# First block: GLU and k projections 512 features wide, chunks loaded in two pieces, parameters on ScalarE's queue, sinks behind the first convolution input

## The chip, the cores and the metric

The kernel runs on one core of a Trainium2 chip. Its engines are TensorE (PE, matrix products), VectorE (DVE) and ScalarE (ACT) for elementwise work, GpSimd (POOL) and SyncE (SP); SP, ACT and POOL can issue DMAs. The metric is the device time in microseconds (us), median of three runs.

## What is computed

Two transformer blocks on x of 512 tokens by 1024 features, in float32. Only the first block's mixer is touched by the change:

```python
h = rms_norm(x, norm1_g)
proj = h @ w_in                      # 1024 x 2560
q, k, v, glu_a, glu_b = split(proj)  # 512 features each
q = rms_norm(q by head, q_norm_g); k = rms_norm(k by head, k_norm_g)
attn = stick_breaking_attention(q, k, v)        # 8 heads of 64
c = glu_a * sigmoid(glu_b)
c = causal_depthwise_conv(c, conv_dw_w, conv_dw_b)   # 31 taps
c = silu(layer_norm(c, conv_ln_g, conv_ln_b))
x = x + concat([attn, c]) @ w_out
```

After it come a gated feed-forward with a 3-tap convolution, then a second block with its own mixer (gated recurrence and sliding-window attention with sinks), a second gated feed-forward and a last norm. The sinks are read by the second block alone.

## The kernel before

Every product is made of float32r parts: a weight chunk arrives as `raw`, ScalarE casts it to `whi`, VectorE takes the rest as `wlo`; the normed input has parts `n_hi` and `n_lo`; `mm3` issues three matmuls for each pair (hi*hi, hi*lo, lo*hi). `WeightStream.load` issues the DMA on SP and records the two splits; there are 3 buffers for `raw` and 4 each for `whi` and `wlo`, and `get` loads up to three chunks ahead. Weights lie in memory in the order of use, which `weight_plan` makes.

A class `Recorder` records all instructions in program order and then orders them by list scheduling on estimated costs: each engine takes the first instruction in program order whose operands and buffers are there. The result is a fixed order for every engine's queue; on the chip each engine runs its queue in that order, so an instruction that waits holds all behind it. Tiles of one tag ("lane") share `BUFS` buffers: lane `x` has 8, lane `z` has 4 PSUM banks, `mm` 2, `o` 1.

The first block's steps stand in `ORDER1`: `glu0 glu1 k1 taps2 taps0 k0 q0 v conv0 stick0 q1 conv2 ...`. At the start SP loads x in eight tiles of 128 features (256 KB each), and `AFTER_X` says after which of them a weight chunk is recorded. `Norm.add` makes `n_hi` on ScalarE and `n_lo` on VectorE for each tile, scaled by `gain1`, a tile of 8 columns that ScalarE's own queue loads; the other parameters (`prm`, 361 columns, 180.5 KB) come later, on SP. `square` sums the squares for the norm.

`glu(c)` makes 256 of the 512 channels: `project_quarter` gives token-major halves, [128 tokens, 256 features] in half a PSUM bank, first for the gate (`glub`), then for the value (`glua`); sigmoid on ScalarE and a product on VectorE follow, four transposes (`gluT`) by channel tile, and a copy into `cpad` (ScalarE). `qk_quarter` does four heads of q or k in the same half-bank form: copies `tn`, squares, sums by head (`ms`), a reciprocal square root by logarithm and one Newton step (`u`, `r`), a product with `tn`, transposes, `qn`/`kn`.

The convolution has two helpers. `conv_taps` makes the first taps by ScalarE products `tap` that GpSimd adds by accumulating DMAs onto one tile per channel tile, 13 in a row for tiles 0 and 1 and 2 for tiles 2 and 3; each product lies in a buffer of lane `x` until its DMA has landed. `conv_pair` does the other taps on VectorE (`conv`), then adds the sums of the first. `stick_pair` (steps stick0 to stick3) needs `e` tiles, also of lane `x`: scores on PE (`z`), three activations, a maximum and split on VectorE (`sph`, `spl`), sums on PE, weighted values (`av`). `conv_norm` (`cmu`, `cvar`) ends the convolution path; then the output product `wo` starts with that part.

The sinks, 4 KB, are loaded by GpSimd:

```python
sink = cp.tile([P, 8], F32, name="sink")
G.dma_start(sink, sinks_2.partition_broadcast(P).rearrange("p o h -> p (o h)"))
```

It needs nothing, so its place is the start of GpSimd's queue.

## Time and profile before

| | |
|---|---|
| runs | 1208.17, 1208.4, 1210.71 us; median 1208.4 |
| span of the profiled execution, first to last instruction | 1205.9 us |
| TensorE busy | 1191.8 us, 6144 matmuls |
| VectorE busy | 761.3 us, 1288 instructions |
| ScalarE busy | 504.1 us, 795 instructions |
| GpSimd busy | 32.4 us, 85 instructions |
| weights and x on SP's queue | 105.65 MB |

The profile gives the span as the execution's only time; the median of the runs lies 2.5 us above it. All times below are us from the span's start unless they are durations. A matmul's busy time includes its flow through the array, so consecutive ones overlap; the distance of starts tells what one costs.

### The profile page before, as it was taken

What the parts mean: (1) busy time and instruction counts of PE and PEld (TensorE: products, weight loads), DVE (VectorE), ACT (ScalarE), POOL (GpSimd) and SP (SyncE); (2) the same over time, 40 slices, a digit from 0 to 9 for tenths busy, and PEclk for the clock granted to TensorE, in tenths of its full rate; (3) what the DMA queues carried; (4) which work ended last, traced back from release to release, by engine and by line L of the source; (5) the groups of instructions that cost most, each with busy time, mean ns of one, the idle gap of its engine ahead of it and who ended that gap; (6) DMA issues with size and microseconds to landing.
All of it is one profiled execution on the core that took longest, in us unless ns stands there. A gap on an engine that the chain in (4) does not pass through costs nothing.

```text
span 1205.9 us, 15657 instructions
## 1 busy us (share of the span) xinstructions
PE 1191.8 (99%) x6144; PEld 988.7 (82%) x6144; DVE 761.3 (63%) x1288; ACT 504.1 (42%) x795; POOL 32.4 (3%) x85
## 2 busy tenths in 40 slices
PE   9999999999999999999999999999999999999997
PEld 8998766888888888888889877778888888888886
DVE  6889885676653566355775667877666445653554
ACT  7286796453321233133544245655523223321324
POOL 0033100000000000000000000000000000000000
PEclk9999999999999999999999999999999999999999
DMA  7389421233232323322322222112332323232321
GB/s 235 106 181 200 92 88 35 77 99 105 88 105 88 105 90 103 92 96 79 118 70 72 70 78 68 49 61 79 105 100 92 104 89 105 88 105 89 103 71 70
DMA packets 36553, 116.09 MB, mean 96 GB/s; under 512 B 4224, under 2 KB 4352, under 8 KB 36480
## 3 DMA queue, kind: packets, MB, share of 16 engines
q1 hardware_dynamic: 31248, 105.65, 28.1%
q0 software_dynamic: 4512, 8.39, 4.0%
q8 instruction: 48, 0.79, 0.3%
q10 hardware_dynamic: 720, 1.05, 0.2%
q14 instruction: 25, 0.20, 0.1%
HBM read 105.12 MB, written 2.10 MB: 89 GB/s over the span
## 4 chain that ended last, share of the span: by engine, by line
PE 94%; DMA 3%; DVE 1%; ACT 1%; issue 0%; SPq 0%; ACTq 0%; POOLq 0%
PE d L266 20%; PE g L266 20%; PE u L266 20%; PE wo L266 7%; PE z L266 4%; DMA tap<-tap 2%; PE hi L266 2%; PE glub L266 2%; PE hg L266 2%; PE glua L266 2%; PE hq L266 2%; PE hf L266 2%; PE aq L266 2%; PE hl L266 2%; PE av L266 1%; PE k0ps L266 1%
## 5 line engine op out<-in xcount | busy, mean ns | idle before, releaser
L266 ACT CAST whi<-raw 128x1024 fp32r<-128x1024 f32 (+2 forms) x194 | 200.8, 1035 | 475.2 <-PE d L266 152.1
L266 DVE TENSOR_TENSOR wlo<-raw,whi 128x1024 fp32r<-128x1024 f32 (+2 forms) x194 | 233.0, 1201 | 93.7 <-ACT whi L266 93.4
L266 PE MATMUL g<-n_hi,whi 128*128 128x512 f32 x352 | 137.2, 390 | 0.0
L266 PE MATMUL g<-n_hi,wlo 128*128 128x512 f32 x352 | 137.1, 390 | 0.0
L266 PE MATMUL g<-n_lo,whi 128*128 128x512 f32 x352 | 137.1, 389 | 0.0
L266 PE MATMUL u<-n_lo,whi 128*128 128x512 f32 x352 | 137.0, 389 | 0.0
L266 PE MATMUL u<-n_hi,whi 128*128 128x512 f32 x352 | 137.0, 389 | 0.0
L266 PE MATMUL u<-n_hi,wlo 128*128 128x512 f32 x352 | 137.0, 389 | 0.0
L266 PEld LDWEIGHTS u<-n_hi,whi 128*128 128x128 f32 x352 | 66.1, 188 | 13.8
L266 PEld LDWEIGHTS u<-n_hi,wlo 128*128 128x128 f32 x352 | 66.1, 188 | 13.7
L266 PEld LDWEIGHTS g<-n_hi,wlo 128*128 128x128 f32 x352 | 66.1, 188 | 13.7
L266 PEld LDWEIGHTS g<-n_hi,whi 128*128 128x128 f32 x352 | 66.1, 188 | 13.7
L266 PEld LDWEIGHTS u<-n_lo,whi 128*128 128x128 f32 x352 | 66.1, 188 | 13.6
L266 PEld LDWEIGHTS g<-n_lo,whi 128*128 128x128 f32 x352 | 66.1, 188 | 13.5
L266 DVE TENSOR_TENSOR s<-s,u 128x512 f32<-128x512 f32 x44 | 30.3, 688 | 67.1 <-PE u L266 67.1
L266 DVE TENSOR_TENSOR gp<-g,n__rstd 128x512 f32<-128x512 f32 x44 | 30.4, 692 | 63.9 <-PE g L266 63.8
L266 PE MATMUL d<-wlo,f_hi 128*128 128x512 f32 (+1 forms) x182 | 69.5, 382 | 0.0
L266 PE MATMUL d<-whi,f_lo 128*128 128x512 f32 (+1 forms) x182 | 69.5, 382 | 0.0
L266 PE MATMUL d<-whi,f_hi 128*128 128x512 f32 (+1 forms) x182 | 69.5, 382 | 0.0
L266 PE MATMUL d<-f_hi,whi 128*128 128x512 f32 x176 | 68.5, 389 | 0.0
L266 PE MATMUL d<-f_lo,whi 128*128 128x512 f32 x176 | 68.5, 389 | 0.0
L266 PE MATMUL d<-f_hi,wlo 128*128 128x512 f32 x176 | 68.5, 389 | 0.0
(389 smaller groups left out, 2388.6 us busy)
## 6 DMA issues: line engine op xcount, KB each, us to landing
raw<-in_weights_dram SPq DMA_DIRECT2D x182, 512.0 KB, 3.6
tap<-tap POOLq DMA_DIRECT2D x30, 256.0 KB, 4.7
raw<-in_weights_dram SPq DMA_DIRECT2D x8, 384.0 KB, 3.1
xin<-in_x_dram SPq DMA_DIRECT2D x8, 256.0 KB, 6.2
xres<-in_x_dram SPq DMA_DIRECT2D x8, 256.0 KB, 3.4
raw<-in_weights_dram SPq DMA_DIRECT2D x4, 256.0 KB, 5.7
out_dram<-hts ACTq DMA_DIRECT2D x4, 256.0 KB, 2.8
out_dram<-hts SPq DMA_DIRECT2D x4, 256.0 KB, 2.6
```

Of the source, the lines that this page charges most:

```text
L266: getattr(self.engines[op.queue], method)(*op.args, **op.kw)
```

## The change

The GLU becomes one product 512 features wide for each `c`: 256 columns of the gate and 256 of the value side by side, in four full PSUM banks of lane `z`, for both `c`. A chunk then consists of two pieces that lie apart in the weights, each with a DMA, a cast and a subtraction of its own into halves of one `whi` and one `wlo` tile. `GLU` sets the chunks: for `glu0` one 128-row block each for the first two, then two each; for `glu1` two each. `raw` still has 3 buffers, now counted in pieces. k becomes one product of 512 features (chunks of two blocks, as v has), with one norm over 32 columns where there were two over 16; q stays in quarters. `ORDER1` has `k` in place of `k1`, and no `k0`. The whole of `prm` is loaded first, on ScalarE's queue, in place of `gain1`, and SP's later load of it is gone. `AFTER_X` goes from (0, 2, 4, 6) to (0, 1, 3, 5). The sinks' DMA waits for the first `cpad` tile. The tiles `sq` go from lane `t` to lane `a`. The diff, without lines that only drop comments:

```diff
-AFTER_X = (0, 2, 4, 6)
+AFTER_X = (0, 1, 3, 5)
...
-ORDER1 = "glu0 glu1 k1 taps2 taps0 k0 q0 v conv0 stick0 q1 conv2 stick1 cnorm stick2 wo0 stick3 wo1 wo2 wo3".split()
+GLU = [[(0, 1), (1, 1), (2, 2), (4, 2), (6, 2)], [(0, 2), (2, 2), (4, 2), (6, 2)]]
+ORDER1 = "glu0 glu1 k taps2 taps0 q0 v conv0 stick0 q1 conv2 stick1 cnorm stick2 wo0 stick3 wo1 wo2 wo3".split()
...
-        key, _, _, k, _, n = self.plan[i]
-        raw = self.tile("raw", i, k, n, F32, self.bufs[0])
-        size = P * k * n
-        self.dma.dma_start(raw, self.src[self.pos:self.pos + size].rearrange("(p k n) -> p k n", p=P, k=k))
-        self.pos += size
-        hi = self.tile("whi", i, k, n, F32R, self.bufs[1])
-        self.act.copy(hi, raw)
-        lo = self.tile("wlo", i, k, n, F32R, self.bufs[1])
-        self.dve.tensor_sub(lo, raw, hi.bitcast(F32))
+        key, pieces = self.plan[i]
+        k, width = pieces[0][3], sum(piece[5] for piece in pieces)
+        hi = self.tile("whi", i, k, width, F32R, self.bufs[1])
+        lo = self.tile("wlo", i, k, width, F32R, self.bufs[1])
+        o = 0
+        for j, (_, _, _, _, _, n) in enumerate(pieces):
+            raw = self.tile("raw", f"{i}_{j}", k, n, F32, self.bufs[0])
+            size = P * k * n
+            self.dma.dma_start(raw, self.src[self.pos:self.pos + size].rearrange("(p k n) -> p k n", p=P, k=k))
+            self.pos += size
+            part = [a if n == width else a[:, :, o:o + n] for a in (hi, lo)]
+            self.act.copy(part[0], raw)
+            self.dve.tensor_sub(part[1], raw, part[0].bitcast(F32))
+            o += n
...
     def glu(c):
-        quarter("b", c, 2048, 4 if c else 2)
-        quarter("a", c, 1536)
+        for i, (k, nk) in enumerate(GLU[c]):
+            for c0 in (2048, 1536):
+                plan.append((("glu", c, i), "w_in", k, nk, c0 + 256 * c, 256))
...
-    gain1 = cp.tile([P, KD], F32, name="gain1")
-    A.dma_start(gain1, params[:, 0:KD])
+    A.dma_start(prm, params)
...
-        n1.add(x_in[j], gain1[:, j:j + 1])
+        n1.add(x_in[j], prm[:, j:j + 1])
...
-    SP.dma_start(prm, params)
...
-        for key in ("b", "a"):
-            pss = project_quarter([(key, c, k) for k in range(2 if c or key == "a" else 4)], f"glu{key}{c}", tag)
-            for t in range(4):
-                g, ps = (a[t // 2][:, 256 * (t % 2):256 * (t % 2) + 256] for a in (gates, pss))
...
+        pss = project_tok("z", [("glu", c, i) for i in range(len(GLU[c]))], h, f"glu{c}")
+        for t in range(4):
+            g = gates[t // 2][:, 256 * (t % 2):256 * (t % 2) + 256]
+            A.activation(g, pss[t][:, 0:256], AF.Sigmoid, scale=rt1[:, t:t + 1])
+            V.scalar_tensor_tensor(g, pss[t][:, 256:512], rt1[:, t:t + 1], g, ALU.mult, ALU.mult)
...
-    def qk_quarter(which, c):
+    def qk_heads(which, c, width):
...
+        if width == 512:
+            pss = project_tok("z", [(which, k) for k in range(4)], h, n + "ps")
+        else:
+            pss = project_quarter([(which, c, k) for k in range(2)], n + "ps")
...
-            sq = t_tile(f"{n}sq{i}")
+            sq = a_tile(f"{n}sq{i}")
...
-    G.dma_start(sink, sinks_2.partition_broadcast(P).rearrange("p o h -> p (o h)"))
+    G.dma_start(sink, sinks_2.partition_broadcast(P).rearrange("p o h -> p (o h)"), after=[cpad[0]])
```

How the order of the queues changes is shown at three places. The first is the start of the program, on two queues. SP's queue before, from the first load on (`xin` are the tiles of x, `raw` the weight chunks, `con` the masks):

```order
L266 DMA xin0_72<-in_x_dram 128x512
L266 DMA raw0_75<-in_weights_dram 128x512
L266 DMA xin1_78<-in_x_dram 128x512
L266 DMA xin2_81<-in_x_dram 128x512
L266 DMA raw1_84<-in_weights_dram 128x512
L266 DMA xin3_87<-in_x_dram 128x512
L266 DMA xin4_90<-in_x_dram 128x512
L266 DMA raw2_93<-in_weights_dram 128x512
```

SP's queue after (`raw1_0` and `raw1_1` are the two pieces of chunk 1):

```order
L267 DMA raw0_1_77<-in_weights_dram 128x256
L267 DMA xin1_78<-in_x_dram 128x512
L267 DMA raw1_0_83<-in_weights_dram 128x256
L267 DMA xin2_85<-in_x_dram 128x512
L267 DMA xin3_88<-in_x_dram 128x512
L267 DMA xin4_95<-in_x_dram 128x512
L267 DMA xin5_98<-in_x_dram 128x512
L267 DMA xin6_105<-in_x_dram 128x512
L267 DMA xin7_108<-in_x_dram 128x512
L267 DMA con_123<-in_masks_dram 128x640
L267 DMA raw1_1_84<-in_weights_dram 128x256
L267 DMA con0_125<-in_masks_dram 128x512
```

The second piece of chunk 1 stands behind all of x and the first masks, since `raw` has three buffers. ScalarE's queue at the start, before:

```order
L266 ACTIVATE n1_6_hi_100<-xin6_99,gain1_68 128x512
L266 ACTIVATE n1__sq3_111<-xin3_87 128x512
L266 ACTIVATE n1_7_hi_106<-xin7_105,gain1_68 128x512
L266 ACTIVATE n1__sq4_112<-xin4_90 128x512
L266 CAST whi3_103<-raw3_102 128x512
L266 ACTIVATE n1__sq5_113<-xin5_96 128x512
```

The same place after:

```order
L267 ACTIVATE n1_5_hi_99<-xin5_98,prm_67 128x512
L267 ACTIVATE n1_6_hi_106<-xin6_105,prm_67 128x512
L267 ACTIVATE n1_7_hi_109<-xin7_108,prm_67 128x512
L267 ACTIVATE n1__sq2_113<-xin2_85 128x512
L267 ACTIVATE n1__sq3_114<-xin3_88 128x512
L267 CAST whi1_81<-raw1_1_84 128x256
```

The cast of that second piece, on which PE's matmuls of the second block of x depend, stands behind the last `n_hi` and two squares.

The second place is ScalarE's queue where the taps of channel tiles 0 and 1 begin, before:

```order
L266 ACTIVATE tap0_0_197<-cpad0_147,prm_67 128x512
L266 COPY k1tn0_183<-k1ps0_172 128x512
L266 ACTIVATE tap1_0_198<-cpad1_149,prm_67 128x512
L266 ACTIVATE tap0_1_199<-cpad0_147,prm_67 128x512
L266 ACTIVATE tap1_1_200<-cpad1_149,prm_67 128x512
L266 COPY k1tn1_184<-k1ps1_173 128x512
L266 ACTIVATE k1sq0_185<-k1tn0_183 128x512
L266 ACTIVATE k1sq1_186<-k1tn1_184 128x512
L266 CAST whi15_228<-raw15_227 128x1024
L266 ACTIVATE tap0_2_201<-cpad0_147,prm_67 128x512
L266 ACTIVATE tap1_2_202<-cpad1_149,prm_67 128x512
```

The same place after:

```order
L267 ACTIVATE tap0_0_218<-cpad0_151,prm_67 128x512
L267 ACTIVATE tap1_0_219<-cpad1_153,prm_67 128x512
L267 ACTIVATE tap0_1_220<-cpad0_151,prm_67 128x512
L267 CAST whi14_187<-raw14_0_189 128x1024
L267 ACTIVATE tap1_1_221<-cpad1_153,prm_67 128x512
L267 ACTIVATE tap0_2_222<-cpad0_151,prm_67 128x512
L267 ACTIVATE tap0_4_226<-cpad0_151,prm_67 128x512
L267 CAST whi15_190<-raw15_0_192 128x1024
L267 ACTIVATE tap1_2_223<-cpad1_153,prm_67 128x512
L267 COPY k0tn0_196<-k0ps0_177 128x512
L267 ACTIVATE tap0_3_224<-cpad0_151,prm_67 128x512
```

The product `tap0_4` now stands ahead of `tap1_2` and of `tap0_3`, and k's copies come later in the row of taps.

The third place is VectorE's queue behind the last step of the first convolution pair (`conv0`, `conv1`), before:

```order
L266 SCALAR_TENSOR_TENSOR conv1_284<-cpad1_149,prm_67,conv1_284 128x512
L266 TENSOR_REDUCE k1ms_180<-k1sq0_185 128x8
L266 TENSOR_REDUCE k1ms_180<-k1sq1_186 128x8
L266 TENSOR_TENSOR k1ms_180<-k1ms_180,rt_sq_124 128x16
L266 TENSOR_TENSOR wlo15_229<-raw15_227,whi15_228 128x1024
L266 TENSOR_SCALAR k1ms_180<-k1ms_180 128x16
L266 SCALAR_TENSOR_TENSOR conv2_331<-cpad2_169,prm_67,tap2_0_191 128x512
L266 SCALAR_TENSOR_TENSOR conv3_332<-cpad3_171,prm_67,tap3_0_192 128x512
L266 SCALAR_TENSOR_TENSOR conv2_331<-cpad2_169,prm_67,conv2_331 128x512
L266 SCALAR_TENSOR_TENSOR conv3_332<-cpad3_171,prm_67,conv3_332 128x512
L266 SCALAR_TENSOR_TENSOR conv2_331<-cpad2_169,prm_67,conv2_331 128x512
```

The same place after:

```order
L267 SCALAR_TENSOR_TENSOR conv0_285<-cpad0_151,prm_67,conv0_285 128x512
L267 SCALAR_TENSOR_TENSOR conv1_286<-cpad1_153,prm_67,conv1_286 128x512
L267 TENSOR_TENSOR wlo14_188<-raw14_0_189,whi14_187 128x1024
L267 SCALAR_TENSOR_TENSOR conv2_333<-cpad2_174,prm_67,tap2_0_212 128x512
L267 SCALAR_TENSOR_TENSOR conv2_333<-cpad2_174,prm_67,conv2_333 128x512 x2
L267 SCALAR_TENSOR_TENSOR conv3_334<-cpad3_176,prm_67,tap3_0_213 128x512
L267 TENSOR_TENSOR wlo15_191<-raw15_0_192,whi15_190 128x1024
L267 SCALAR_TENSOR_TENSOR conv3_334<-cpad3_176,prm_67,conv3_334 128x512
L267 SCALAR_TENSOR_TENSOR conv2_333<-cpad2_174,prm_67,conv2_333 128x512
L267 TENSOR_REDUCE k0ms_193<-k0sq0_200 128x8
```

The head sums of four heads of k (`k1ms`) stood here between the two pairs' convolution steps; now the next pair's steps, which need `tap2` and `tap3`, follow at once, and k's first head sum comes behind six of them.

## Rows read from the trace of the kernel before

**Rows 1.** TensorE's waits from 94 to 240 us (engine, line, tile; who ended the wait; us in total, times, longest).

```profile
PE z L266 <- ACT sph L266: 2.1, 1, 2.1
PE z L266 <- DVE spl L266: 0.3, 1, 0.3
```

**Rows 2.** The chain of work that ended last, in order of time: start, us, what. Products of 256 columns (`glub`, `glua`, `k0ps`, `q0ps`), of 512 (`u`), the norm's sums (`n__ss`) and two GLU transposes.

```profile
9.06 12.53 PE glub L266 x90
...
22.55 0.79 PE n__ss L266 x8
23.34 10.66 PE glua L266 x88
...
46.37 11.52 PE glua L266 x96
57.89 0.22 PE gluT L266 x2
...
70.26 11.52 PE k0ps L266 x96
...
85.65 8.53 PE q0ps L266 x71
...
252.80 10.88 PE u L266 x48
```

**Rows 3.** The busy table of stretches: from and to, us, busy time (and instructions) of PE, PEld, DVE, ACT, POOL, then granted clock of TensorE (1.00 is 2.4 GHz, 0.50 is 1.2 GHz), share of the DMA engines, GB/s.

```profile
0.00:3.00 3.00, 1.95 (x9) 1.95 (x10) 0.17 (x2) 1.28 (x1) 1.17 (x9) 1.00 0.37 90
3.00:4.00 1.00, 1.00 (x7) 1.00 (x7) 0.00 (x0) 0.10 (x1) 0.00 (x0) 1.00 0.97 277
4.00:6.00 2.00, 1.99 (x9) 1.70 (x9) 1.07 (x2) 1.65 (x3) 0.00 (x0) 1.00 0.54 62
7.00:9.00 2.00, 0.50 (x2) 0.30 (x2) 0.75 (x2) 1.50 (x3) 0.00 (x0) 1.00 1.05 406
9.75:13.15 3.40, 3.40 (x18) 3.40 (x17) 3.40 (x6) 3.40 (x7) 0.00 (x0) 0.50 1.05 384
```

**Rows 4.** The first loads: the page's list of DMA issues (count, KB, us to landing) for the sinks.

```profile
sink<-in_sinks_dram POOLq DMA_DIRECT2D x1, 4.0 KB, 5.4
```

**Rows 5.** The timeline of the start (start, us, engine, line, operation, tiles, count, in brackets the idle time before it and what ended it).

```profile
1.35 0.68 POOL L266 DMA_DIRECT2D sink<-in_sinks_dram  x1 [0.33 <-issue]
...
3.90 0.72 ACT L266 ACTIVATE n_hi<-xin,gain 128x512 fp32r<-128x512 f32 x1 [1.88 <-DMA gain<-in_params_dram]
...
7.50 0.72 ACT L266 ACTIVATE n_hi<-xin,gain 128x512 fp32r<-128x512 f32 x1 [1.85 <-DMA xin<-in_x_dram]
...
8.27 0.38 PE L266 MATMUL glub<-whi,n_hi 128*128 128x256 f32 x1 [1.34 <-ACT n_hi L266]
...
15.45 1.67 ACT L266 ACTIVATE n__sq<-xin 128x512 f32<-128x512 f32 x3
```

**Rows 6.** ScalarE's groups up to 60 us, shapes apart (count, busy us, mean ns).

```profile
L266 ACT CAST whi<-raw 128x512 fp32r<-128x512 f32 x4 | 2.4, 606 | 0.0
```

**Rows 7.** The tile view of `tap`: GpSimd's issues (min/median/max of the issue, ns, count, first and last start), and min/median/max from issue to landing.

```profile
L266 POOL DMA_DIRECT2D tap<-tap x30: 850/862/1535, 63.7 to 132.8; - x30
...
DMA to landing us min/median/max: 3.3/4.7/6.4
```

**Rows 8.** ScalarE's waits from 60 to 160 us (columns as in rows 1).

```profile
ACT tap L266 <- DMA tap<-tap: 6.4, 8, 2.5
...
ACT e L266 <- DMA tap<-tap: 3.0, 1, 3.0
```

**Rows 9.** The chain of work again, from the taps to the convolution norm's first sum.

```profile
102.41 0.49 issue
102.90 5.58 DMA tap<-tap
...
120.79 6.37 DMA tap<-tap
...
127.26 0.50 ACT e L266
...
130.27 0.33 PE z L266
...
156.68 0.86 PE cmu L266 x2
```

**Rows 10.** The busy table for the matmuls of `q1ps` alone (PE, PEld, then ACT).

```profile
130.27:141.00 10.73, 4.72 (x32) 4.19 (x32) 0.57 (x1) 1.00 0.65 124
```

**Rows 11.** VectorE's timeline at the end of the first convolution pair.

```profile
66.87 1.41 DVE L266 SCALAR_TENSOR_TENSOR conv<-cpad,prm,conv 128x512 f32<-128x512 f32 x2
71.45 1.28 DVE L266 TENSOR_REDUCE k1ms<-k1sq 128x8 f32<-128x512 f32 x2 [3.17 <-ACT k1sq L266]
...
72.91 1.23 DVE L266 TENSOR_TENSOR wlo<-raw,whi 128x1024 fp32r<-128x1024 f32 x1
...
74.12 1.41 DVE L266 SCALAR_TENSOR_TENSOR conv<-cpad,prm,tap 128x512 f32<-128x512 f32 x2
...
80.42 1.30 DVE L266 TENSOR_TENSOR k1tn<-k1tn,k1r 128x512 f32<-128x512 f32 x2
```

**Rows 12.** The busy table of later stretches (columns as in rows 3).

```profile
80.00:100.00 20.00, 20.00 (x150) 18.93 (x150) 18.43 (x33) 14.57 (x26) 7.38 (x9) 1.00 0.87 190
100.00:120.00 20.00, 20.00 (x99) 15.90 (x97) 18.78 (x30) 13.27 (x19) 6.34 (x8) 1.00 0.90 195
120.00:140.00 20.00, 17.92 (x133) 15.60 (x132) 17.34 (x28) 13.14 (x27) 5.58 (x10) 1.00 0.73 144
140.00:176.00 36.00, 35.61 (x170) 20.67 (x168) 30.65 (x67) 33.21 (x71) 0.00 (x0) 1.00 0.18 59
252.00:350.72 98.72, 98.72 (x437) 81.76 (x436) 64.29 (x85) 34.68 (x41) 0.90 (x9) 1.00 0.32 96
```

More of the change, by code (lines that the diff above doesn't have):

```diff
@@ L274, in __init__ @@
         self.dma, self.act, self.dve = (rec.engine(q) for q in ("SP", "ACT", "DVE"))
-        self.pool, self.src, self.plan, self.ahead, self.bufs = pool, src, plan, ahead, bufs
+        self.pool, self.src, self.ahead, self.bufs = pool, src, ahead, bufs
+        self.plan = []
+        for piece in plan:
+            if self.plan and self.plan[-1][0] == piece[0]:
+                self.plan[-1][1].append(piece)
+            else:
+                self.plan.append((piece[0], [piece]))
         self.tiles = {}
@@ L321, in glu, with half @@
     def glu(c):
-        quarter("b", c, 2048, 4 if c else 2)
-        quarter("a", c, 1536)
-    def values1():
+        for i, (k, nk) in enumerate(GLU[c]):
+            for c0 in (2048, 1536):
+                plan.append((("glu", c, i), "w_in", k, nk, c0 + 256 * c, 256))
+    def half(key, c0):
         for k in range(4):
-            plan.append((("v", k), "w_in", 2 * k, 2, 1024, 512))
+            plan.append(((key, k), "w_in", 2 * k, 2, c0, 512))
     def gates(c):
@@ L359, in ffn @@
                     plan.append((("d", b, pt, j), wd, j0, n, P * j, P))
-    steps1 = {"v": values1}
+    steps1 = {"v": lambda: half("v", 1024), "k": lambda: half("k", 512)}
     for i in range(2):
@@ L647, in project_quarter @@
         return pss
-    def qk_quarter(which, c):
-        n = f"{which}{c}"
-        pss = project_quarter([(which, c, k) for k in range(2)], n + "ps")
-        ms, u, r = (s_tile(f"{n}{a}", (P, 16)) for a in ("ms", "u", "r"))
+    def qk_heads(which, c, width):
+        n, per = f"{which}{c}", 512 // width
+        nh = width // 64
+        if width == 512:
+            pss = project_tok("z", [(which, k) for k in range(4)], h, n + "ps")
+        else:
+            pss = project_quarter([(which, c, k) for k in range(2)], n + "ps")
+        ms, u, r = (s_tile(f"{n}{a}", (P, 4 * nh)) for a in ("ms", "u", "r"))
         by_tok = [a.rearrange("p (t h) -> p t h", t=4) for a in (ms, r)]
         tn = []
-        for i in range(2):
+        for i in range(len(pss)):
             t = t_tile(f"{n}tn{i}")
@@ L659, in qk_quarter @@
             tn.append(t)
-        for i in range(2):
-            sq = t_tile(f"{n}sq{i}")
+        for i in range(len(pss)):
+            sq = a_tile(f"{n}sq{i}")
             A.activation(sq, tn[i], AF.Square)
             V.tensor_reduce(ms[:, 8 * i:8 * i + 8], sq.rearrange("p (a d) -> p a d", d=64), AX.X, ALU.add)
-        V.tensor_mul(by_tok[0], by_tok[0], rt_sq.unsqueeze(2).to_broadcast([P, 4, 4]))
+        V.tensor_mul(by_tok[0], by_tok[0], rt_sq.unsqueeze(2).to_broadcast([P, 4, nh]))
         V.tensor_scalar(ms, ms, 1.0 / 64, EPS, ALU.mult, ALU.add)
@@ L670, in qk_quarter @@
         V.scalar_tensor_tensor(r, u, 1.5, r, ALU.add, ALU.mult)
-        V.tensor_mul(by_tok[1], by_tok[1], rt1.unsqueeze(2).to_broadcast([P, 4, 4]))
-        for i in range(2):
+        V.tensor_mul(by_tok[1], by_tok[1], rt1.unsqueeze(2).to_broadcast([P, 4, nh]))
+        for i in range(len(pss)):
             t = tn[i].rearrange("p (a d) -> p a d", d=64)
             V.tensor_mul(t, t, r[:, 8 * i:8 * i + 8].unsqueeze(2).to_broadcast([P, 8, 64]))
-        for i in range(2):
+        for i in range(width // P):
             ps = ps_tile("ss", f"{n}T{i}")
             for t in range(4):
-                o = 256 * (t % 2) + P * i
-                PE.transpose(ps[:, t * P:(t + 1) * P], tn[t // 2][:, o:o + P], ident)
-            t = q_tile(f"{which}n{2 * c + i}")
+                o = width * (t % per) + P * i
+                PE.transpose(ps[:, t * P:(t + 1) * P], tn[t // per][:, o:o + P], ident)
+            j = width // P * c + i
+            t = q_tile(f"{which}n{j}")
             A.activation(t, ps, AF.Copy, scale=qg if which == "q" else kg)
-            qk[which][2 * c + i] = t
+            qk[which][j] = t
     BANKS = [[(2, 0), (3, 256)], [(1, 0)], [(0, 0)]]
```

11 lines of the change are left out of this document (2 added, 9 removed).

## The prediction

> **What bounds the kernel now.** I read the chain of waits first, then the waits of TensorE, then the busy table stretch by stretch. The chain is PE nearly throughout, and PE's waits between 94 and 240 us sum to 2.4 us [rows 1], so it looks as if every microsecond taken from PE were won. The change touches only the first 100 us of that. From 252 us on PE streams 512-wide products back to back [rows 2, 12], the same ones after the change, so the end moves by what the last part of the first block's mixer moves.
>
> There the busy table tells something else. From 140 to 176 us PE is shown busy for 35.61 of 36 us, but its weight loads fill 20.67, against 81.76 of 98.72 in the feed-forward, while ScalarE is busy for 33.21 and VectorE for 30.65 [rows 12]. PE there mostly flows out short products between answers of two nearly full engines. And the chain runs through accumulating DMAs of the taps until 127 us, and only then into the first `e` of the stick-breaking attention [rows 9]. So there are three runners into this stretch: PE, the tap chain, and VectorE's convolution sums. The shortest time needs all three to come earlier.
>
> The Trainium skill, page Trainium Kernel Development and Optimization, section Performance Expectations, says that matmul busy time is a bad measure of how near a kernel is to its limit, and that the busy share of weight loads is a good one. The trace agrees: 99% against 57% in that stretch; this bears on the chance of the first rival.
>
> **Part 1, wider products.** 96 products of 256 columns take 11.52 us, 120.0 ns each; 48 of 512 take 10.88, 226.7 each [rows 2]. The GLU and k are six quarters of 96, 576 x 120.0 = 69.12 us; after, 288 x 226.7 = 65.28. PE has 3.84 us less to do, 2.56 of it in the GLU and 1.28 in k.
>
> The Trainium skill, page TensorE: Matmul & The Clock Gate, section "Wait — 56ns, not 53.3ns?", puts the fixed part of a matmul at about 2.5 ns on top of columns / 2.4 GHz. By that, an estimate, two of 256 cost 218.3 and one of 512 costs 215.8, and the change would save 0.7 us. The rows show 2 x 120.0 - 226.7 = 13.3 ns, so here the measurement decides.
>
> **Part 2, the start.** Three things move. (a) The sinks: their 4 KB are issued at 1.35 and need 5.4 us [rows 4, 5], and while they are under way, from 4 to 6 us, all loads together get 62 GB/s, against 277 before and 406 after [rows 3]; the second x tile is used only at 7.50 [rows 5]. Behind the first `cpad` they lie at some 36 us, where nothing of SP's queue is short; on GpSimd only the taps' DMAs stand behind them, 27 us later. That gives the start 0.69 MB back (2 us at 406 less 62 GB/s). Cover gone, one chunk would come 1.7 us late. (b) `prm`, 0.185 MB, shares the DMA engines with the first x tile: 0.185 / 0.406 = 0.46 us, so the first `n_hi` starts at 4.4 for 3.90 [rows 5]. If it came far later still, nothing below would change, because of (c).
>
> (c) PE works through blocks in order, and block 1 needs both pieces of chunk 1. The second is the 13th load of SP's queue. Up to it 8 x tiles, 4 pieces of 128 KB, the masks' 320 KB and `prm` move: 2.097 + 0.524 + 0.328 + 0.185 = 3.134 MB. By 4.0 us 0.547 MB are there (3 x 90 + 277 [rows 3]); the rest at 406 GB/s takes 6.4 us, so 10.4. From arrival to use I add 0.9, as the first tile shows (0.27 MB by 3.0, used at 3.90): 11.3. Its cast stands behind the last `n_hi` and two squares. The last x tile is there at 4.0 + 2.128 / 0.406 + 0.9 = 10.1; then 0.72 and 2 x 0.56 [rows 5] lead to 11.9, and the cast of half the width of a 0.606 one [rows 6], between 0.3 and 0.6, say 0.4, to 12.3. So PE does 12 matmuls by some 9.5, stands until 12.4, and has 84 of the first GLU before it: 84 x 0.2267 = 19.0. Before, PE waited 1.34 and more at 8.27 [rows 5] and then got half the clock from 9.75 to 13.15 [rows 3], which cost 3.40 / 2 = 1.7 us; with a wait twice as long I charge the same once. With the norm's sums, 0.79 [rows 2]: 12.4 + 19.0 + 1.7 + 0.8 = 33.9. Now it is 23.34 + 10.66 = 34.0 [rows 2]. The first `cpad` comes no earlier: what the sinks and the wider products give is spent on waiting for that piece.
>
> From there PE gains. Second GLU: 33.9 + 21.76 + 0.88 for eight transposes (0.22 for two [rows 2]) = 56.6, for 57.89. k: + 0.88 + 21.76 = 79.2, for 81.78. q0 with k's transposes: 91.6, for 94.2. So PE leads by 2.6 us, and no other term of the sum can make more of it.
>
> More casts: 18 pieces for 10 on ScalarE and as many subtractions on VectorE, about 1.2 us each, beside PE's 40 us of GLU, where both have room; pieces of 256 KB halve what three `raw` buffers hold, but two blocks are 5.4 us of PE and a piece lands within that. Costed at nothing; if the cover failed, a fraction of a microsecond per chunk.
>
> **Part 3, the tap chain.** 30 DMAs from 63.7 to 132.8 [rows 7], 13 in a row for tiles 0 and 1, each 4.7 to landing [rows 7] and 0.5 to the next issue [rows 9]. It begins when the second GLU is done, so it starts 1.3 earlier at best and runs at its own pace. But ScalarE's order has `tap0_4` before `tap1_2`; it needs a buffer of lane `x` that comes free when VectorE has read `tap3`. Such waits now total 6.4 us, the longest 2.5 [rows 8]. `tap1_2` and tile 1's whole chain stand behind it: 0 to 2.5, I take 2.0, since it comes at once where the lane is full. Net +0.7 (-1.3 to +1.2) at the first `e` of 127.26 [rows 9]. PE's lead ends there in waiting: by then it has only q1 to fill with.
>
> **Part 4, VectorE.** At 68.3 the first pair ends, VectorE waits 3.17 us, and then works off the norm of four heads of k between 71.45 and 81.7 [rows 11]: 1.28 for sums, 1.30 for products, some 0.6 for eight small ones, 3.2 us in all, while the taps of the next pair land. After, k is whole only at 79.2, so this fill is gone and 3.2 us of work move behind 80, where VectorE is busy for 18.4 and 18.8 of 20 us [rows 12]. That leaves little to take it up: 0 (all idle time to 140 us is used) to 3.2, I take 2.8, by the 6% that are free between 100 and 120. It delays the convolution sums and `cmu` (156.68 [rows 9]), and each VectorE step of the attention queued among them.
>
> **Part 5, the attention's waits.** After 130.27 q1 still covers PE's waits with 32 matmuls, 3.8 us [rows 10]. With the lead they lie before it, and nothing covers. That shifts work, it takes none, so PE's waits open: 0 to 2.1 (the one now seen, 2.1 [rows 1], once more), I take 1.1.
>
> **Sum.** +0.7 + 2.8 + 1.1 = +4.6 us on the profiled span, 1205.9 to 1210.5. The span lies 2.5 us under the median of the runs, 1208.4, and what lies around it doesn't change: **1213.0 us**. About 0.2% (2.4 us) is what a measurement of this kernel can tell from no change.
>
> **Rivals.** *PE keeps the end:* the other two have slack, and the lead of 2.6 reaches the end: 1205.8. For it speak the chain and PE's 2.4 us of waits; against it ScalarE at 33.21 of 36. It decides if the tap chain gets its 1.3 and VectorE takes up the 3.2. By the Trainium skill's 2.5 ns (page and section as above) the lead would be 2.6 - 3.1, below nothing, and this case 1208.9. *The tap chain alone:* VectorE's idle time of 5.5 us between 80 and 140 [rows 12] takes up the moved work, q1's fill isn't missed: +0.7, 1209.1. *A worse start:* PE stands longer at block 1, the half clock is granted for a second such stretch, 1.7 more, and the first `cpad`, the taps and VectorE's chain all shift; with the upper bounds 1.2 + 3.2 + 2.1 it comes to +8.2, 1216.6. The sinks or `prm` failing to do what they say would not show, since neither is what PE waits for last.
>
> **How the numbers follow.** Forecast 0.48, tap chain alone 0.19, PE keeps the end 0.13, worse start 0.20. Slower 0.48 + 0.20 = 0.68, same 0.19, faster 0.13. The range reaches from the first rival's time, 1205.8, over the worse start to 1218.0; that leaves out half of the first rival and what lies beyond the upper bounds.
>
> **What would show it.** Right: a wait of PE of about 3 us before 12.4 for `whi`, the first `cpad` at 34 to 36, k's last product near 79; the last tap DMA no earlier than now; a longer idle time of VectorE at 68 to 74 and `cmu` 3 us later; PE waits for `sph`, `spl` and `e` between 130 and 180 of 6 us or more. Wrong: `cmu` at or before 156 with fewer such waits, or a second wait of PE of over 1 us before 40.

## The result and the profile after

| | before | after |
|---|---|---|
| runs | 1205.1 to 1210.71 us, median 1208.29 (4 runs) | 1216.16 to 1219.74 us, median 1218.32 (4 runs) |
| ratio, 95% interval | | 1.0081 (1.006 to 1.0102) |
| span of the profiled execution | 1205.9 us | 1215.6 us |

The changed kernel is 10 us slower, where +4.6 was forecast: the sign was right, the size was not, and the time lies just above the range. One execution of all that follow, the profiled one of the variant e15, took 3055.9 us, two and a half times the others, so e15's median is over the other eleven and it has no rows. Line 267 is here what line 266 is in the kernel before.

**The start.** The timeline of the changed kernel (columns as in [rows 5]):

```profile
1.36 0.68 POOL L267 DMA_DIRECT2D sink<-in_sinks_dram  x1 [0.34 <-issue]
...
7.50 0.72 ACT L267 ACTIVATE n_hi<-xin,prm 128x512 fp32r<-128x512 f32 x1 [1.69 <-DMA xin<-in_x_dram]
...
8.57 1.51 PE L267 MATMUL glu<-whi,n_hi 128*128 128x512 f32 x3 [2.98 <-ACT whi L267]
...
13.98 0.39 ACT L267 CAST whi<-raw 128x256 fp32r<-128x256 f32 x1
...
14.42 1.20 PE L267 MATMUL glu<-whi,n_hi 128*128 128x512 f32 x4 [1.25 <-ACT whi L267]
...
37.26 0.59 ACT L267 COPY cpad<-gluT 128x512 f32<-128x512 f32 x1 [0.84 <-PE gluT L267]
```

TensorE's first product of the kernel before, from the same view:

```profile
5.70 0.78 PE L266 MATMUL glub<-whi,n_hi 128*128 128x256 f32 x2
```

The sinks' DMA has not moved: 1.36 us for 1.35 in [rows 5], and the second x tile is used at 7.50 as before. `after=[cpad[0]]` only tells the list scheduler of a need. It changes no place in GpSimd's queue, which holds nothing between the four `cpad` memsets and that DMA, and where an instruction doesn't touch the tile's data the chip gets no wait. TensorE waits twice for pieces of a chunk, 3.0 us until 8.57 and 1.25 until 14.42. The first wait is that of its first product, which needs both pieces of chunk 0: the second one's cast stands behind the second `n_hi` (7.50) in ScalarE's queue. Before, the first product started at 5.70. The piece that ends the second wait was cast at 13.98. ScalarE wasn't idle just before it, so the cast was held by its place behind the `n_hi` and squares, not by its load. The first `cpad` stands at 37.26; before it was 35.78.

**From the first `e` to the last 128 products of `wo`.** The busy table by these two milestones, first of the kernel before, then of the changed one (columns as in [rows 3]):

```profile
127.26:212.21 84.95, 82.48 (x419) 54.01 (x418) 62.55 (x120) 70.42 (x141) 3.95 (x9) 1.00 0.24 63
```

```profile
130.53:221.79 91.26, 85.56 (x419) 55.44 (x417) 62.38 (x119) 70.47 (x143) 3.51 (x9) 0.96 0.21 58
```

419 matmuls in both, VectorE busy for 62.5 and 62.4 us, ScalarE for 70.4 and 70.5. The work is the same and it takes 6.3 us longer. TensorE stands idle for 91.26 - 85.56 = 5.7 us in place of 2.5, and its granted clock is 0.96 in place of 1.00. With the first `e` 3.3 us late (130.53 for 127.26) that is the whole loss of 9.6; behind it the two run alike. More stretches of the changed kernel, the first and third beside [rows 3] and [rows 12], the others at half clock:

```profile
4.00:6.00 2.00, 1.59 (x8) 1.39 (x7) 1.13 (x3) 1.55 (x3) 0.00 (x0) 1.00 0.91 130
8.76:12.17 3.41, 3.41 (x9) 2.64 (x9) 3.41 (x7) 3.41 (x7) 0.00 (x0) 0.50 1.05 392
97.51:100.92 3.41, 3.41 (x11) 2.46 (x10) 3.41 (x6) 1.66 (x3) 1.71 (x2) 0.50 0.65 109
140.00:176.00 36.00, 31.75 (x142) 18.69 (x140) 23.38 (x51) 27.66 (x60) 0.00 (x0) 0.91 0.20 64
145.29:148.71 3.42, 3.42 (x12) 1.92 (x12) 2.66 (x5) 2.97 (x6) 0.00 (x0) 0.50 0.02 5
158.95:162.36 3.41, 3.36 (x16) 2.53 (x17) 2.27 (x9) 1.77 (x5) 0.00 (x0) 0.50 0.00 0
```

In the kernel before, every row of [rows 12] stands at 1.00; its half clock fell at the start (9.75 to 13.15 [rows 3]). What TensorE waits for between 60 and 251 us (columns as in [rows 1], where two lines stood):

```profile
PE k0T L267 <- DVE k0tn L267: 2.3, 1, 2.3
PE z L267 <- DVE e L267: 1.5, 2, 1.1
PE z L267 <- ACT sph L267: 1.1, 2, 0.9
PE z L267 <- DVE spl L267: 1.0, 2, 0.6
PE z L267 <- ACT e L267: 0.9, 1, 0.9
PE q1T L267 <- DVE q1tn L267: 0.8, 1, 0.8
...
```

**How k's norm came to stop TensorE, and the chain.** The chain of work, in order of time:

```profile
88.38 5.89 DMA tap<-tap
94.27 0.02 issue
94.29 0.72 ACT tap L267
95.01 0.53 ACT q0sq L267
95.54 0.02 issue
95.56 0.69 DVE q0ms L267
96.25 0.61 DVE k0tn L267
96.86 0.04 issue
96.90 0.33 PE k0T L267
...
112.63 8.44 PE vps L267 x37
...
123.72 11.10 PE q1ps L267 x92
```

ScalarE's `tap` waits for a DMA; the squares of q0 stand behind it, VectorE's sum of them behind those, k's product `k0tn` behind that, and TensorE has its transposes of k at the head of its queue. Half clock follows at 97.51. At the end, 92 of q1's 96 products lie in one row ahead of the attention's first sums; before, 32 lay behind them [rows 10].

The taps of the changed kernel in the tile view (the last DMA is issued at 138.2; before, at 132.8 [rows 7]):

```profile
L267 POOL DMA_DIRECT2D tap<-tap x30: 850/859/917, 65.0 to 138.2; - x30
```

The last sum of the convolution norm on VectorE and the product that reads it, from the timelines of the kernel before and of the changed one:

```profile
145.57 0.69 DVE L266 TENSOR_TENSOR cacc<-cacc,conv 128x512 f32<-128x512 f32 x1
...
156.52 1.02 PE L266 MATMUL cmu<-cacc,ones 128*128 128x512 f32 x2
```

```profile
146.97 0.69 DVE L267 TENSOR_TENSOR cacc<-cacc,conv 128x512 f32<-128x512 f32 x1
...
167.04 1.07 PE L267 MATMUL cmu<-cacc,ones 128*128 128x512 f32 x2
```

VectorE's sums are late by 1.4 us only. `cmu` is late by 10.5 since TensorE comes to its place in the queue that much later.

### The profile page after: what moved, and what is told of

It is laid out like the page before. It is cut to its first block, busy times and chain, and to the rows that moved or that the text cites. A ratio compares the mean times of both kernels' runs of the same rounds, so it can differ in the third digit from the quotient of the medians.

```text
span 1215.6 us, 15108 instructions
## 1 busy us (share of the span) xinstructions
PE 1193.1 (98%) x5856; PEld 974.7 (80%) x5856; DVE 761.1 (63%) x1288; ACT 506.0 (42%) x803; POOL 32.3 (3%) x85
## 4 chain that ended last, share of the span: by engine, by line
PE 92%; ACT 3%; DMA 2%; DVE 2%; issue 0%; SPq 0%; POOL 0%; POOLq 0%; ACTq 0%
PE d L267 20%; PE g L267 20%; PE u L267 20%; PE wo L267 7%; PE glu L267 3%; PE z L267 3%; PE hi L267 2%; PE hg L267 2%; DMA tap<-tap 2%; PE hq L267 2%; PE hf L267 2%; PE aq L267 2%; PE vps L267 2%; PE hl L267 2%; PE av L267 1%; PE q1ps L267 1%
## 5 line engine op out<-in xcount | busy, mean ns | idle before, releaser
L267 ACT CAST whi<-raw 128x1024 fp32r<-128x1024 f32 (+3 forms) x202 | 201.9, 1000 | 479.3 <-PE d L267 152.2
L267 DVE TENSOR_TENSOR wlo<-raw,whi 128x1024 fp32r<-128x1024 f32 (+3 forms) x202 | 233.8, 1158 | 97.0 <-ACT whi L267 96.1
```

The lines of the kernel that those rows point to most:

```text
L267: getattr(self.engines[op.queue], method)(*op.args, **op.kw)
```

## The experiments

Theory K: k as one product carries the loss. S: the start carries it. O: no part carries it; each edit makes the scheduler write another order for the attention. All runs in one table; "first e" to "cmu" are starts in one profiled execution (us), "clock" is the mean granted clock over the runs. The kernel before had 1207.55 to 1208.86 us beside them, at a clock of 0.996 to 0.997. The ratio compares whole sets of runs; where a difference of medians says something else (e6, e9, e13), the ratio and its interval decide.

| run | us | ratio (95%) | clock | first cpad | last tap DMA | first e | cmu |
|---|---|---|---|---|---|---|---|
| before | | | 0.996 | 35.8 | 132.8 | 127.3 | 156.5 |
| after | 1218.3 | 1.0081 (1.006, 1.0102) | 0.994 | 37.3 | 138.2 | 130.5 | 167.0 |
| e1 | 1214.0 | 1.0046 (1.003, 1.0062) | 0.994 | 37.0 | 136.2 | 129.0 | 160.2 |
| e2 | 1212.6 | 1.0031 (1.0014, 1.0048) | 0.994 | 35.5 | 132.3 | 126.8 | 160.5 |
| e3 | 1215.9 | 1.0057 (1.0037, 1.0077) | 0.992 | 34.3 | 131.9 | 126.3 | 161.5 |
| e4 | 1219.4 | 1.0093 (1.0074, 1.0111) | 0.991 | 36.2 | 137.5 | 130.0 | 168.4 |
| e5 | 1212.3 | 1.0035 (1.0019, 1.0051) | 0.994 | 36.7 | 135.3 | 128.0 | 170.5 |
| e6 | 1221.0 | 1.0084 (1.0053, 1.0116) | 0.991 | 40.6 | 138.7 | 131.6 | 169.8 |
| e7 | 1208.7 | 1.0011 (0.999, 1.0033) | 0.995 | 32.9 | 129.5 | 121.4 | 159.7 |
| e8 | 1209.8 | 1.0009 (0.9993, 1.0025) | 0.996 | 32.5 | 129.6 | 120.9 | 158.8 |
| e9 | 1213.4 | 1.0061 (1.0039, 1.0083) | 0.995 | 36.4 | 136.4 | 129.3 | 161.5 |
| e10 | 1207.1 | 0.9994 (0.9982, 1.0006) | 0.998 | 32.9 | 128.5 | 122.3 | 158.8 |
| e11 | 1207.6 | 1.0002 (0.9991, 1.0013) | 0.997 | 32.8 | 130.4 | 123.5 | 158.3 |
| e12 | 1205.9 | 0.9988 (0.9973, 1.0003) | 0.997 | 31.5 | 128.4 | 121.6 | 156.4 |
| e13 | 1216.5 | 1.0078 (1.0056, 1.0099) | 0.993 | 36.6 | 131.2 | 123.6 | 162.5 |
| e14 | 1220.5 | 1.0102 (1.0075, 1.0128) | 0.990 | 36.1 | 139.9 | 132.4 | 159.4 |
| e15 | 1205.0 | 0.9976 (0.9964, 0.9988) | 0.998 | | | | |
| e16 | 1205.3 | 0.9979 (0.9967, 0.9992) | 0.998 | 30.9 | 127.8 | 119.1 | 157.0 |
| e17 | 1205.3 | 0.9974 (0.9954, 0.9994) | 0.998 | 32.9 | 129.5 | 123.9 | 153.2 |
| e18 | 1208.3 | 0.9996 (0.9981, 1.0011) | 0.995 | 31.2 | 131.6 | 123.1 | 158.8 |

The milestones are those of one execution and move from one to the next: before, e3 and e14 have the same start, and their first `cpad` lies between 34.3 and 36.1. A half-clock stretch at the start, which before and e14 have and e3 has not, makes part of that. The profiled execution needn't be a middle one either: e2's is 4.1 us under the median of e2's runs, e5's 6.4 above; the clock column is over all runs.

### One part undone, one part alone

**e1**, k as quarters again:

```diff
-ORDER1 = "glu0 glu1 k taps2 taps0 q0 v ..."
+ORDER1 = "glu0 glu1 k1 taps2 taps0 k0 q0 v ..."
```

> The changed kernel with k as two quarters of 256 columns again, in their old places among the steps; the wide GLU, the parameters first and the sinks as in the change. Theory K (k as one product carries the loss: VectorE's fill at 71 to 81 us is gone, k's norm stands behind q0, the tap chain and the first e come 3.3 us later): most of the 10 us comes back, 1209 to 1212, the PE wait of 2.3 us for k0tn near 97 and the half clock right behind it are gone, the last tap DMA lands near 138. Theory S (the start carries it: the second piece of chunk 1 is queued behind x and the masks): no more than 3 us come back, 1215 to 1218. Theory O (no part carries it; the order that the list scheduler writes for the attention differs with every edit, and the wins and losses are made there): any value from 1208 to 1220, with new PE waits for sp and e between 130 and 190 us that neither k nor the start explains.

4.3 us come back, less than K's 6 to 9 and more than S's 3. The wait for `k0tn` is gone (one of 1.1 us for ScalarE's copy of k stands there now), the last tap DMA 2 us earlier. k is a part of the loss, under a half.

**e2**, the GLU as quarters again, the rest as changed:

```diff
-AFTER_X = (0, 1, 3, 5)
+AFTER_X = (0, 2, 4, 6)
-pss = project_tok("z", [("glu", c, i) for i in range(len(GLU[c]))], h, f"glu{c}")
+for key in ("b", "a"):
+    pss = project_quarter([(key, c, k) for k in range(2 if c or key == "a" else 4)], f"glu{key}{c}", tag)
```

> The changed kernel with both GLUs as quarters of 256 columns again (and weight chunks behind x tiles 0, 2, 4, 6 as before); k stays one product of 512 columns, the parameters stay first. Theory S: the start's loss is gone, 1209 to 1212. Theory K: 1215 to 1218, with the wait for k0tn and the tap chain's late end as in the change. Theory O: anything from 1208 to 1220. The first cpad should come at 34 to 36 us by all of them.

5.7 us come back, and the first `cpad` is at 35.5. So undoing either gives back about half.

**e3**, the kernel before with k alone as one product:

```diff
-ORDER1 = "glu0 glu1 k1 taps2 taps0 k0 q0 v ..."
+ORDER1 = "glu0 glu1 k taps2 taps0 q0 v ..."
```

> The kernel before with k alone as one 512 wide product (start, GLU, parameters and sinks as before; the squares of q and k in lane a as in the change). Theory K: most of the loss is here without the rest, 1214 to 1217. Theory S: 1207 to 1209 (1.28 us less PE work, nothing else). Theory O: anything, and the sum with the other parts does not add up to 10.

+7.1 us with a start and a tap chain that are no later than before: K's number, while in the change k was worth 4.3. The clock of its runs is among the lowest.

**e5**, the kernel before with the parameters in one first load, and **e6**, with the GLU alone:

```diff
-A.dma_start(gain1, params[:, 0:KD])
+A.dma_start(prm, params)
```

> The kernel before with the last part of the change alone: all parameters in one load, first on ScalarE's queue (and the sinks' DMA recorded as needing the first cpad, which moves it in no queue, and the squares of q and k in lane a). GLU and k as quarters. If the parts add up: 0.46 us at the start and nothing else, 1207 to 1210, and k (7.1 alone) plus this should be what k with the parameters gave, 3.8, so they would have to give back 3.3: 1205. If each edit draws a new order of the attention and a new set of half-clock stretches (theory O): up to 4 us either way, with the difference found between 130 and 241 us and not before 60.

> The kernel before with the GLU alone as 512 wide products from chunks of two pieces (k as quarters, the gains first and the parameters behind x as before). Theory S: the split pieces make TensorE stand at chunk 1, some 2.7 us more idle time before 60 us than before, of which the 2.56 us of less work give most back there; then the tap chain starts 1 us late: 1209 to 1213. Theory K: 1206 to 1208, the lead of 2.56 less the start's loss. Theory O: 1208 to 1216, with the difference made after 130 us.

+4.5 and +13.3 by the medians, 4.2 and 10.1 by the ratios (e6's six runs lie between 1211 and 1223 us). With k's 7.1 (6.9) the three make 25 (21), not 10: the parts don't add, as O said, but each part alone is a loss, and e6 shows the one at the start at its largest. The busy table of e6, at its half-clock stretches beyond the first:

```profile
19.36:26.19 6.83, 6.83 (x21) 5.48 (x20) 4.33 (x9) 3.69 (x9) 0.00 (x0) 0.50 0.67 194
138.83:155.90 17.07, 16.60 (x53) 10.59 (x52) 11.98 (x20) 10.28 (x20) 1.03 (x4) 0.50 0.36 111
```

That is the mechanism of my rival "a worse start", in a kernel that has only the GLU.

### The start, mended

**e4**, the changed kernel with sinks that wait for data:

```diff
-G.dma_start(sink, ..., after=[cpad[0]])
+G.tensor_copy(sink, cpad[0][:, 30:38])
+G.dma_start(sink, ...)
```

> The changed kernel with the sinks' DMA made to wait in earnest for the first cpad tile, by a copy of 8 of its columns into the sink tile ahead of the DMA (0.2 us of GpSimd; the DMA writes over it). Nothing else moves in any queue. Expected by my sum for the start: the sinks' DMA at 37 us in place of 1.36, the dip of the loads to about 62 GB/s between 4 and 6 us gone, the second x tile used 1.7 to 2 us earlier, PE's second wait for whi ended by 12.5 in place of 14.4, the first cpad at 35.3 to 36 in place of 37.3. If that lead is kept to the end, 1216.3; theory K: since the end is set by VectorE and the tap chain, the taps start 1.7 us earlier and the lead is kept or half kept, 1216 to 1218; theory S: 1215 to 1216.5, since an earlier start also shifts the clock's low stretches. Rival: the dip belongs to the start of the queues and not to the sinks' DMA; then it stays and so does the time.

The busy table of e4:

```profile
4.00:6.00 2.00, 1.45 (x8) 1.25 (x7) 1.17 (x3) 1.55 (x3) 0.00 (x0) 1.00 0.98 275
```

and its second wait for a piece, from the timeline:

```profile
13.39 1.20 PE L267 MATMUL glu<-whi,n_hi 128*128 128x512 f32 x4 [1.29 <-ACT whi L267]
```

275 GB/s for 130, so the dip is the sinks' own; the first `cpad` comes 1.1 us earlier. The second wait still ends at 13.39, not by 12.5. In e9 and e13, which have the sinks early and the start of the changed kernel, it ends at 13.53 and 13.77; so at most 1.0 of the 2.0 us by which my 12.4 was too early is the sinks'. The time is the same within its interval, at a lower clock: this lead is lost.

**e7**, whole GLU chunks in the changed kernel:

```diff
-for c0 in (2048, 1536):
-    plan.append((("glu", c, i), "w_in", k, nk, c0 + 256 * c, 256))
+plan.append((("glu", c, i), "w_in", k, nk, (2048 + 256 * c, 1536 + 256 * c), 512))
```

> The changed kernel with the two column ranges of a GLU chunk laid side by side in the weights array, so that a chunk is one load, one cast and one subtraction of 512 columns in place of two of each (9 loads for 18). The amount moved and the products stay. If the start's stall comes from the second piece of a chunk waiting for a raw buffer behind x and the masks: TensorE's idle time before 60 us falls from 5.4 to 3 or less, the GLU ends 2 to 3 us earlier. By theory S the end then comes near the kernel before, 1207 to 1210. By theory K the wait for k0tn, the longer VectorE wait at 71 to 83 and the late cmu stay, 1213 to 1217. By the account of TensorE (end = work + idle time + half the half-clock stretches): what idle time and stretches are left is what the end shows, 1209 to 1214. Rival: more weight per load delays the first product and the start gains nothing.

S's number: 9.6 of the 10 us are back by the medians, 8.5 by the ratios, with k still one product; twelve runs spread from 1204.7 to 1217.7. TensorE's waits up to 60 us in e7, against 4.2 for `whi` in the changed kernel:

```profile
PE warm L267 <- DVE eps L267: 1.1, 1, 1.1
PE glu L267 <- ACT whi L267: 0.5, 1, 0.5
```

No run keeps the pieces and adds buffers for `raw`, so how much of this is the buffers and how much the number and places of loads and casts isn't told apart.

**e8**, the same in another order:

```diff
-"glu0 glu1 k taps2 taps0 q0 v conv0 stick0 q1 conv2 stick1 cnorm stick2 ..."
+"glu0 glu1 k q0 taps2 taps0 v conv0 stick0 q1 conv2 cnorm stick1 stick2 ..."
```

> As the one above, and two steps in other places of the program: q0 ahead of the taps (so that the norms of k and q0 stand ahead of the taps in every engine's queue) and the layer norm of the convolution ahead of the second head pair (so that cmu stands earlier in TensorE's queue). Same work. If the order of the queues between 80 and 180 us carries the loss and not the wide products: cmu some 10 us earlier than in the changed kernel, no wait for k0tn, half-clock stretches gone there, and the end at 1202 to 1208, at or under the kernel before. If VectorE's and ScalarE's work in the attention carries it whatever the order: 1210 to 1216.

Nothing more. But the edit hardly did what it was for: beside e7, `cmu` comes 0.9 us earlier (158.8 for 159.7), and the wait for `k0tn` is still there (1.4 us for 2.1). So this order doesn't help, and whether another would (theory O in its strong form) stays untested.

**e10**, the edits of e7 and e1 together:

> The changed kernel with whole GLU chunks (one load, one cast, one subtraction of 512 columns) and k as two quarters in their old places. Beside the run with whole chunks and k as one product (1208.7) this tells what k as one product costs once the start is mended. Theory K: 3 to 5 us less, 1204 to 1206. Theory S (the start alone, k as one product is worth its 1.28 us or nothing): 1208 to 1210. Theory O: anything within 5 us, with the difference behind 120 us.

1.6 us under e7, the intervals overlap: between K and S.

### The stretch from 120 to 180 us

**e9**, products with zeros where TensorE waits, in the changed kernel:

```diff
+for hd in heads:
+    PE.matmul(pss[hd, b][:, :n], zero_r, con_r[:, :n], start=False, stop=False)
 for hd in heads:
     sums(b, hd)
```

> The changed kernel with 12 more products in the first two head pairs of the attention, 128 rows by 256 to 512 columns of a matrix of zeros, added to each score bank between the softplus that reads it and the sums that wait for its parts: that is where TensorE waits. They add nothing to the scores and 12 x 0.2 us or a little less of TensorE work (2.5 us). Theory C (the granted clock is a cause: thin work between waits lets it fall to half, each stretch costs up to 1.7 us): the half-clock stretches between 130 and 190 us get fewer, the granted clock of the runs rises, and the time is the same or falls, 1213 to 1218. Theory W (the waits alone cost, the half clock falls where TensorE waits anyway and costs nothing): the stretches may go, but the time rises by what does not fit into waits, 1218 to 1221.

With 2.5 us more of TensorE work it is 4.9 us faster by the medians, but 2.4 by the ratios, and the two intervals overlap (from 1.0039 and 1.006 up): that it is faster isn't clear of the noise, that it isn't slower by the added work is likely. The profiled execution, the fastest of seven, has no half clock between 130 and 190 us. That leans to C. But the zero matrix also moves the scheduler's order, and this execution had no half clock at the start either, so what the clock did here isn't settled.

**e11**, whole chunks, k's quarter for heads 4 to 7 behind v, and **e12**, the same with sinks that wait as in e4:

```diff
-"glu0 glu1 k1 taps2 taps0 k0 q0 v conv0 stick0 q1 ..."
+"glu0 glu1 k0 taps2 taps0 q0 v conv0 k1 stick0 q1 ..."
```

> As the one above, but with the quarter of k that heads 4 to 7 need taken out of the stretch before v and put behind v, beside q1: 96 products of 120 ns that nothing needs before the third head pair, so that TensorE has 11.5 us more full work between 115 and 150 us, and the taps and the first heads start earlier relative to it. Same work in all. If the lead of the wide GLU is lost because TensorE has too little full work among the answers of VectorE and ScalarE (waits and half clock there): fewer stretches of half clock between 130 and 190 us, idle time there under 2.5 us, 1202 to 1206, under the kernel before. If VectorE's and ScalarE's own work sets the stretch: 1207 to 1211.

> As the one above, and the sinks' DMA made to wait in earnest for the first cpad tile. The order of every queue but GpSimd's is the same. By the run with late sinks alone the first cpad comes 1.1 us earlier. If a lead of TensorE and of the taps at 35 us is kept to the end when the attention has full work: 0.5 to 1.2 us less than the one above. If it is lost there again: the same or up to 2 us more, with more half-clock stretches.

e11 is e10's time: more full work there gives nothing once the chain is early. e12 is 1.7 us under e11 (0.5 to 1.2 expected), as if the lead of late sinks were kept; the intervals overlap.

**e13**, the changed kernel with one tap less in the two chains, and **e14**, the kernel before with one more:

```diff
-TAPS = (14, 3)
+TAPS = (13, 3)   # e13; e14: (15, 3)
```

> The changed kernel with 13 taps of the first two tiles by ScalarE and accumulating DMAs in place of 14 (two DMAs less in the two chains, two multiply-adds of 0.6 us more on VectorE). Tap chain as the runner: its last DMA lands some 5 us earlier, at 136 to 137, the first e at 125 to 127, and the end falls to 1209 to 1213. VectorE as the runner: the last DMA lands earlier all the same, cacc comes 1 us later, and the end stays at 1217 to 1221.

> The kernel before with 15 taps in the two chains in place of 14 (two DMAs more, two multiply-adds of 0.6 us less on VectorE); start, GLU and k as before. It makes the chain late without touching the start: last DMA at 142 to 144, first e at 130 to 133. Tap chain as the runner: 1213 to 1220, with half-clock stretches behind 130 us as in the changed kernel, though TensorE's start is as before. VectorE as the runner: 1206 to 1209.

e14 costs 12 us though its start is that of before: a chain that ends 7 us later is enough to make a loss as large as the change's. Its busy table at a stretch of half clock:

```profile
139.33:146.16 6.83, 6.77 (x24) 4.29 (x24) 6.07 (x15) 4.74 (x12) 1.03 (x4) 0.50 0.54 96
```

e13 shows that it is not the chain alone: the first `e` comes 6.9 us earlier, and the end gains 1.8 by the medians, 0.4 by the ratios, nothing clear of the noise. VectorE has the two taps now, and its last sum starts at 151.28 in the timeline of e13, 4.3 us later than in the changed kernel:

```profile
151.28 0.69 DVE L267 TENSOR_TENSOR cacc<-cacc,conv 128x512 f32<-128x512 f32 x1
```

So chain and VectorE look both near their limit.

### What the wide GLU and the sinks are worth

**e15** and **e17**, the kernel before with the edit of e4, **e16**, e10 with it, **e18**, e7 with it:

> The kernel before with the sinks' DMA behind the first cpad in earnest (a copy of 8 columns of that tile ahead of it), nothing else changed. The first cpad 1.0 to 1.7 us earlier (34.1 to 34.8). If the end follows the start of the tap chain: 1206.5 to 1207.5. If the attention's stretch takes the lead away: 1208 to 1209. Less than 1206.3, the full 2 us of my sum, by neither.

> The kernel before with late sinks once more, for its rows. If the gain is the start's: the loads' dip between 4 and 6 us is gone, TensorE's first wait for n_hi ends 1 to 2 us earlier, the first cpad is at 33.8 to 34.8 and the last tap DMA lands 1 to 2 us before 138.0; the time is 1204.5 to 1206.5. If it is the clock's: the first cpad comes less than 0.7 us earlier, and there is one half-clock stretch less.

> GLU as 512 wide products from whole chunks, k as two quarters in the old places, parameters first, sinks late in earnest. Beside the same without late sinks (1207.1): 1205 to 1206.5 if a lead at the start is kept, 1207 to 1208.5 if it is lost in the attention. Beside the kernel before: the wide GLU's 2.56 us are worth 1 to 3 us by this run, or nothing.

> The changed kernel with whole GLU chunks and the sinks late in earnest, k as one product. By the runs so far: 1208.7 with whole chunks, less 1.2 to 1.7 for the sinks where the start bounds: 1207.0 to 1207.5, 0.6 to 1.2 us under the kernel before. With k as two quarters it was 1205.3; if k as one product costs nothing, 1205 to 1206; if it costs 2 us or more through VectorE, 1207.3 and up.

e15 and e17 are each about 3.6 us faster than the kernel before by the medians, 2.9 and 3.1 by the ratios, more than I had expected. The busy table of e17, beside the same three stretches of [rows 3]:

```profile
4.00:6.00 2.00, 1.97 (x10) 1.68 (x9) 1.05 (x2) 2.00 (x4) 0.00 (x0) 1.00 1.03 329
7.00:9.00 2.00, 2.00 (x17) 1.82 (x16) 1.81 (x4) 2.00 (x5) 0.00 (x0) 1.00 1.04 381
9.75:13.15 3.40, 3.40 (x30) 3.40 (x29) 3.40 (x7) 3.40 (x7) 0.00 (x0) 1.00 1.05 394
```

The dip is gone, and with it the wait of 1.34 us. The half clock behind that wait is gone too: 30 products between 9.75 and 13.15 in place of 18. But that isn't shown to be the sinks' doing. e3 has the sinks early and nearly the same wait (1.25 us), and no half clock follows it:

```profile
9.75:13.15 3.40, 3.40 (x31) 3.40 (x30) 3.40 (x6) 3.40 (x7) 0.00 (x0) 1.00 1.05 383
```

The first `cpad` is at 32.91, 2.9 earlier, the first `e` 3.3, `cmu` 3.3: when all runners come earlier together, the lead reaches the end whole. Beside e3, which has no half clock at the start either, the sinks give 1.4 us at the first `cpad`; e16 beside e10, e18 beside e7 and e12 beside e11 say 1.9, 1.7 and 1.3.

e16 has the wide GLU too, 2.56 us less work, and the same time as e17. It also loads the parameters first, which alone cost 4.5 us in e5, so it doesn't isolate the width. e18 has k as one product as well and is 2 (by the ratios) to 3 us (by the medians) slower than e16, with intervals that overlap; TensorE's wait for `k0tn` is there again, 3.5 us.

## Why the prediction was wrong

**Part 1 held.** In the chain of the changed kernel 92 products of 256 take 11.10 us and 37 of 512 take 8.44: 2 x 120.7 - 228.1 = 13.3 ns saved for a pair, as the rows had said and not the 2.5 ns that the Trainium skill (page TensorE: Matmul & The Clock Gate, section "Wait — 56ns, not 53.3ns?") gives as the fixed part.

**Part 2 is the step that failed.** (a) I took the diff at its word that the sinks go behind the first `cpad`; the DMA stayed at 1.36, and the 0.69 MB that I gave back to the start never came. I had written that this failing would not show; at the end of the changed kernel it doesn't (e4), at the first `cpad` it is 1.1 us. (c) I had one wait, for the second piece of chunk 1, and charged it against what the sinks and the width give. There were two: the first product itself needs two pieces and started at 8.57, where I had 12 products done by 9.5, and the second piece of chunk 1 came at 14.4 in place of 12.4, in e4 with late sinks at 13.4. Beyond that I costed the pieces "at nothing; if the cover failed, a fraction of a microsecond per chunk". Whole chunks (e7) bring the first `cpad` from 37.3 to 32.9 and the time back by 9.6 us (8.5 by the ratios): of all single edits to the changed kernel the largest, where I had no term. Two pieces of each chunk take two of three `raw` buffers, and the second one's load and cast stand behind x and the squares.

**Part 3 was mis-sized** by what part 2 left out: the first `e` came 3.3 us late, not 0.7. The taps start 1.3 us later (65.0 for 63.7) in place of 1.3 earlier. The rest lies in the chain itself; with k as quarters (e1) the first `e` is 1.5 earlier.

**Part 4 was right in the place and wrong in the form.** VectorE took up the moved work: its last `cacc` is 1.4 us late, not 2.8. What I hadn't seen of k as one product is TensorE's wait for `k0tn`, 2.3 us: k's norm now stands behind q0's squares, and those behind a tap's DMA. It isn't the whole cost: alone k costs 7.1 (e3), where that wait is 1.4, so the rest stays open. With the start mended k costs some 2 (e7 beside e10, e18 beside e16; the intervals overlap).

**Part 5 was right in kind and too small.** Nothing of q1 is left behind the first sums, and TensorE's idle time from the first `e` on rises by 3.2 us (1.1, at most 2.1 forecast). Half clock there was in no term: two stretches, 6.8 us, up to 3.4 us of time. 3.3 + 3.2 + 3.4 = 9.9, against 9.6 measured up to the feed-forward.

**The rivals.** "A worse start" (1216.6) comes nearest: a second wait of over 1 us before 40, and a later chain with the upper bounds behind it. But its second half-clock stretch didn't fall at the start; it fell at 97, 145 and 159 us. "PE keeps the end" did not come true, and e7 speaks against it: its first `cpad` is 2.9 us ahead of the kernel before and its end is not (1.0011). Of the signs I named, a wait of 3 us for `whi` was there, but for chunk 0; the last tap DMA no earlier and the longer idle time of VectorE were there. The first `cpad` (34 to 36) and k's last product (79; it ended at 80.8) were not, `cmu` was 10 us later, not 3, and TensorE's waits for `sph`, `spl` and `e` between 130 and 180 came to 3.9 us, not 6 or more.

**What stays open.** Over these kernels the time goes with the runs' granted clock: 0.998 at 1205.0 to 1207.1, 0.990 to 0.991 at 1219.4 to 1221.0. 0.001 of clock is 1.2 us of a span of 1208 at most, and the difference in time is about twice that, so the clock carries at most about half and waits come with it. Which of the two starts it in each stretch, the runs don't tell apart; e9 only leans to the clock.
